# A decoder layer on one core: a fixed order of ScalarE and VectorE where attention begins, an earlier start of the first norm's sums, and another order in the closing chain

## The chip, the core and the metric

One core of a Trainium2 chip runs the whole layer in one launch. The metric is device time in microseconds (us), the median of several executions. The engines are TensorE (PE, matrix products), VectorE (DVE), ScalarE (ACT), GpSimd (POOL) and SyncE (SP, whose queue issues most transfers). Each executes its own instructions strictly in the order in which they were laid down, and waits at the first one whose inputs or buffers aren't ready.

## The reference

One decoder layer on 512 tokens of width 1024, all in 32-bit floats:

```python
cs = silu(c);  shift1, scale1, gate1, shift2, scale2, gate2 = split(cs @ w_ada + b_ada, 6)
h = rmsnorm(x, norm1_g) * (1 + scale1) + shift1
qa, ka, va, qd, kd, vd, ga, gd = split(h @ w_in)
out_a = sliding_window_attention(qa, ka, va, sinks)      # 8 heads, 2 key heads, window 128, ALiBi
out_d = diff_attention(qd, kd, vd, lambda)               # 4 heads, two softmax maps each, ALiBi
merged = sigmoid(ga) * (out_a @ w_branch_swa) + sigmoid(gd) * (out_d @ w_branch_diff)
x = x + gate1 * (merged @ w_out)
h2 = rmsnorm(x, norm2_g) * (1 + scale2) + shift2
x = x + gate2 * conv_ffn(h2)                             # up 1024 -> 2 x 2816, conv of 3, GELU, down
out = rmsnorm(x, final_g)
```

## The kernel before

Products are made to near 32-bit accuracy from two halves of each operand: a rounded high part (written by ACT, a cast or scaled copy) and the low part, the rest (written by DVE, a subtraction). A product is three matmuls: high by high, high by low, low by high. `split_pair` (L105) does it for a weight tile, `keep_v`, `stack` and `evac` for results that leave PSUM; `stack` puts the high and low half of one 64-row head above each other, so that one matmul multiplies both. Where a block is under `tc.manual_schedule(engines=...)`, the engines named run its instructions in the order of the text; elsewhere a scheduler orders them by priority and a model of their times, and `tc.issue_after(ins)` ties what a block issues on the engine of `ins` behind it.

**The opening** (L199 to L390, a fixed order on all engines). SP loads x in four quarters, then for each of eight slices k of the width two slabs of `w_ada` (the `adaw` tiles) and one of the first weights (`w0`). ACT squares each quarter of x, DVE folds the square in two, and `sums` (L289) adds over the partitions on PE, with a matrix of ones, into `stat`. `csb` is silu(c) spread over all partitions, copied from PSUM by two DVE copies (L253, L298). The shift's and scale's row sums are DVE multiply-and-reduce instructions (`mod_rows`, L259); for slice 0 the scale's is made by PE instead (`head_mod`, L279). ACT loads the root's table (`root_table`, L165), takes the root (L304), DVE finishes it (L306 on), PE turns it to a row (L312), and `scale_x`, `mod` and `h_tile` make h (L322, L357, L328). `keep_warm` puts products of constants into PE's idle time. Then PE multiplies slice after slice (`mm_k`, L339 and L342) into eight PSUM banks `acc[0..7]`: key (0), two query pairs (1, 2), values (3, 4, 6, 7 for the token blocks), window values (5). In the last slice the order of the banks is written out, so that they end one after the other.

**Where attention begins** (L434 on). ACT and DVE empty the eight banks: `keep_v(3)`, four copies of the key (L443) and two subtractions (L445), the first query pair (`stack`, L415 on ACT, L418 on DVE), copies of the key's low part, `vaT`; these are in a fixed order. The second query pair and the other three `keep_v` are not. PE's order is fixed: `fill(n)` does n steps (three matmuls each) of a queue of projections still to be done, the first two being query pairs 2 and 3 from weight tiles `wqa2` and `wqa3`, and between fills come the attention steps: `swa_scores` (L540, two calls for a pair; maxima on DVE, L545), `swa_softmax`, `swa_transpose`, `swa_values`. `SWA_FILL` lists the fills between them: the first before the first scores, the second between the two calls. Scores use the three banks tagged `s`, projections the two tagged `f`, transposes the two tagged `t`; `acc` holds the same banks before. `load_tile` issues a tile's transfer and its cast and low part; `prefetch` keeps one or two tiles ahead.

**Merge and output projection** (L884 to L1190). `add_merge(j)` finishes merged column block j on DVE (L913, L914 and a split). `load_rows` loads eight slabs of `w_out` (`wo`), multiplies each with the gate on DVE (L961) and splits it. The projection's eight accumulators (`oc`, L1186 to L1190) take the same PSUM banks as the merges' sums.

**The closing chain** (`last_rows`, L1671 on, fixed order on all engines). For the last two rows of tokens, u = 0 and 1, the half that is still open is multiplied by the gate (`last_mul`, L1648), added (`last_add`, L1651), squared (`last_square`, L1656), the root is taken (`root_start`, `root_end`), and both halves are scaled and written out (`last_final` L1664, `last_scale2` L1668). Row 1 is done in two quarters, c0 and c1, since PE ends with c1 in a bank of its own, `dY[1]`.

Of the kernel before, what the change touches and what calls it, by code (L numbers as in the profile page):

```python
# [8 lines left out]
F32 = mybir.dt.float32  # L9
# [5 lines left out]
P = 128  # L15
# [19 lines left out]
VA_AT = 5  # L35
SWA_FILL = (1, 2, 6, 2, 2, 2, 2, 3)
DIFF_FILL = (3, 2, 4, 2)
# [6 lines left out]
def kernel(  # L44
# [207 lines left out]
    nc.vector.tensor_mul(cb, bsc1, n1g)  # L252
    nc.vector.tensor_copy(csb[:, :S], acc[0])  # L253

# [19 lines left out]

    NB = P

    def head_mod(a0, a1):
# [6 lines left out]
    stat = acc[6][:, : NT * NB].rearrange("p (t n) -> p t n", n=NB)  # L284
    keep_warm(2)

    def sums(p):
        for t in range(NT):
            nc.tensor.matmul(  # L289
                stat[:, t], sqs[p][:, t * P : (t + 1) * P], ones[:, :NB], start=p == 0 and t == 0, stop=True,  # L290
                skip_group_check=True,
            )

    sqs = [pp.tile([P, 2 * S], F32, tag="sq", bufs=4, name=f"sq{p}") for p in range(KT // 2)]
    for p in range(KT // 2):
        nc.scalar.activation(sqs[p], xT[:, p], AF.Square)
        if p == 3:
            nc.vector.tensor_copy(csb[:, S:], acc[1])  # L298
        nc.vector.tensor_add(sqs[p][:, :S], sqs[p][:, :S], sqs[p][:, S:])
# [9 lines left out]
    rstd_end(rst, ms, r0, NT, pp)  # L309
    head_mod(0, 6)  # L310
    for t in range(NT):
        nc.tensor.transpose(acc[7][:, t * P : (t + 1) * P], rst[:, t : t + 1].to_broadcast([P, P]), ident)  # L312
# [6 lines left out]
    ALL = slice(0, S)  # L319

# [33 lines left out]
    HALVES = (slice(0, S // 2), slice(S // 2, S))  # L354
    scale_x(0, HALVES[0])
    m = mods[0]
    nc.vector.tensor_scalar(m[:, 0:1], acc[3][:, 0:1], n1g[:, 0:1], cb[:, 0:1], ALU.mult, ALU.add)  # L357
    nc.vector.tensor_add(m[:, 1:2], m[:, 3:4], bsh[:, 0:1])
    scale_x(0, HALVES[1])
# [49 lines left out]

    def stack(dst, src, scale, js=(0, 1), soon=True):  # L410
        with tc.high_priority(offset=HP) if soon else ExitStack():
            sc = [scale if isinstance(scale, float) else scale[own] for own, _ in halves]
            for j in js:
                own = halves[j][0]
                nc.scalar.activation(dst[own, j], src[own], AF.Copy, scale=sc[j])  # L415
            for j in js:
                own, other = halves[j]
                nc.vector.scalar_tensor_tensor(  # L418
                    dst[other, j], src[own], sc[j], dst[own, j].bitcast(F32), ALU.mult, ALU.subtract
                )  # L420
# [12 lines left out]

    def keep_v(i):  # L434
        t = TOKENS[i] * P
        evac(*(v[:, :, t : t + P] for v in vv), acc[i].rearrange("p (h d) -> p h d", d=P))

    man = ExitStack()
    man.enter_context(tc.manual_schedule(engines={nc.vector.engine, nc.scalar.engine}))
    keep_v(3)  # L440
    for j, (own, other) in enumerate(halves):
        for to in (own, other):
            nc.scalar.copy(ka[to, j, 0], acc[0][own])  # L443
    for j, (own, _) in enumerate(halves):
        nc.vector.tensor_sub(ka[own, j, 1], acc[0][own], ka[own, j, 0].bitcast(F32))  # L445
# [20 lines left out]


    def load_tile(n, name):
        r = raw_tile([P, KT, P], name)
        nc.sync.dma_start(r, w_tiles[n])  # L470
        return split_pair(r, [P, KT, P], name)

# [126 lines left out]
    def add_q(i):  # L599
        def q(wts):  # L600
            o = fbank(f"pqa{i}")
            yield from steps(o, wts, hT, KT)
            stack(qa[:, i], o, qsc[:, i : i + 1])

        units.append((lambda: load_tile(TILE_QA + i, f"wqa{i}"), q))

# [159 lines left out]
    ada = ada_rows()  # L766
    add_q(2)
    add_q(3)
# [95 lines left out]
    tdall = gpart(2, [P, 3, S], "tdall")  # L864
    tds = {}

# [26 lines left out]
    def add_merge(j):  # L893
# [14 lines left out]
        def branch(wts):  # L908
            o = sbank(f"pB{j}")
            rhs = [[vv[b][:, k] for k in range(4)] for b in range(2)]  # L910
            yield from steps(o, wts, rhs, 4, cl=slice(j % 2 * P, j % 2 * P + P))
            td = tds[j]
            nc.vector.scalar_tensor_tensor(td, td, 1.0, o, ALU.add, ALU.mult)  # L913
            nc.vector.tensor_add(td, td, ta[:, j])  # L914
            split(mgh[j], mgl[j], td)
# [755 lines left out]
    def last_rows(todo):  # L1671
# [132 lines left out]
```

## Time and profile before

| | us |
|---|---|
| median of 3 runs | 684.09 |
| lowest, highest | 683.17, 686.54 |
| profiled execution, whole | 684.12 |
| its span, first to last instruction | 682.3 |
| busy in it: PE, DVE, ACT, POOL | 670.2, 567.7, 403.7, 66.1 |

The profiled execution's time is 1.8 us more than its span. PE's busy time counts pipelined matmuls from start to a modelled end, so it hides short waits between them; where PE waits is better read from how many matmuls lie in a stretch.

### The profile page before, as it was taken

To read this page: it belongs to the slowest core of one execution; us is meant where nothing else is said; L and a number is where in the kernel's file an instruction comes from. 1 tells how busy PE (TensorE), PEld (TensorE's weight loads), DVE (VectorE), ACT (ScalarE), POOL (GpSimd) and SP (SyncE) were. 2 spreads that over 40 slices of the span, in tenths; PEclk is the share of its full clock that TensorE was granted. 3 is DMA by queue.
4 is the path that set the end of the run, shared out by engine and by line. 5 is a ranking of instruction groups with operands and counts; after the bars stand their busy time and mean duration, and the time that the engine had idled before them with its cause. 6 is when DMAs were issued, how large, how long until landed. Compare 5 with 4: busy or idle time off the path is not lost.

```text
span 682.3 us, 10835 instructions
## 1 busy us (share of the span) xinstructions
PE 670.2 (98%) x4053; PEld 594.3 (87%) x4053; DVE 567.7 (83%) x1049; ACT 403.7 (59%) x703; POOL 66.1 (10%) x74
## 2 busy tenths in 40 slices
PE   8999999999999999999999999999999999999995
PEld 7887787888888888878899999999999998888884
DVE  5986887789887388973689998888888999979997
ACT  6678878565654233332498565565556666656665
POOL 2000000001000000000020120111110003440300
PEclk9999999999999999999999999999999999999998
DMA  9961322354254289757473998787867658996903
GB/s 359 418 218 35 124 62 94 123 155 130 93 180 155 80 291 304 263 128 270 144 125 97 215 218 213 185 194 178 215 159 189 149 185 189 195 204 188 166 1 124
DMA packets 71077, 119.68 MB, mean 175 GB/s; under 512 B 3952, under 2 KB 47728, under 8 KB 71024
## 3 DMA queue, kind: packets, MB, share of 16 engines
q1 hardware_dynamic: 52960, 95.04, 41.7%
q0 software_dynamic: 17776, 23.60, 21.4%
q8 instruction: 32, 0.52, 0.3%
q10 hardware_dynamic: 288, 0.34, 0.2%
q14 instruction: 21, 0.17, 0.1%
HBM read 116.87 MB, written 2.10 MB: 174 GB/s over the span
## 4 chain that ended last, share of the span: by engine, by line
PE 79%; DVE 8%; DMA 6%; issue 3%; ACT 3%; ACTq 0%; DVEq 0%
PE up L1130 33%; PE dc L1733 11%; DMA wgd<-in_w_tiles_dram 3%; PE av L342 3%; DMA wo<-in_w_out_dram 2%; PE oc L1186 2%; PE oc L1187 2%; PE oc L1190 2%; PE pga L108 2%; PE pga L110 2%; PE pga L109 2%; PE sd L637 2%; PE aqa L339 1%; PE pq L108 1%; PE pk L108 1%
## 5 line engine op out<-in xcount | busy, mean ns | idle before, releaser
L1130 PE MATMUL up<-t,m_whi 128*128 128x256 f32 x512 | 93.1, 283 | 0.0
L1130 PEld LDWEIGHTS up<-t,m_whi 128*128 128x128 f32 x512 | 79.9, 192 | 0.0
L1130 PE MATMUL up<-t,m_wlo 128*128 128x256 f32 x256 | 72.4, 283 | 0.0
L1130 PE MATMUL up<-bh,p_whi 128*128 128x256 f32 x232 | 65.7, 283 | 0.0
L1130 PE MATMUL up<-bl,p_whi 128*128 128x256 f32 x232 | 65.7, 283 | 0.0
L1130 PE MATMUL up<-bh,p_wlo 128*128 128x256 f32 x232 | 65.7, 283 | 0.0
L1130 PEld LDWEIGHTS up<-t,m_wlo 128*128 128x128 f32 x256 | 49.2, 192 | 0.0
L1130 PEld LDWEIGHTS up<-bh,p_whi 128*128 128x128 f32 x232 | 44.5, 192 | 0.0
L1130 PEld LDWEIGHTS up<-bl,p_whi 128*128 128x128 f32 x232 | 44.5, 192 | 0.0
L1130 PEld LDWEIGHTS up<-bh,p_wlo 128*128 128x128 f32 x232 | 44.5, 192 | 0.0
L1033 POOL DMA_DIRECT2D s<-in_w_up_dram x21 | 27.0, 1365 | 158.2 <-DMA s<-in_w_up_dram 110.3
L1061 ACT CAST m_whi<-s 128x1024 fp32r<-128x1024 f32 x31 | 32.4, 1046 | 15.7 <-DVE s L1055 9.1
L732 DVE CUSTOM_DVE_ANT_0 ra<-ra,csb 128x1024 f32<-128x1024 f32 x32 | 38.6, 1221 | 1.6 <-DMA ra<-in_w_ada_t_dram 1.5
L1065 DVE TENSOR_TENSOR m_wlo<-s,m_whi 128x1024 fp32r<-128x1024 f32 x31 | 37.8, 1219 | 1.3 <-ACT m_whi L1061 1.3
L1130 PE MATMUL up<-t,p_whi 128*128 128x256 f32 x176 | 32.2, 283 | 0.0
L662 ACT ACTIVATE sd<-sd,dmx 128x128 f32<-128x128 f32 (+3 forms) x32 | 17.8, 557 | 20.7 <-DVE dmx L660 16.5
L1130 PEld LDWEIGHTS up<-t,p_whi 128*128 128x128 f32 x176 | 27.4, 192 | 0.1
L1061 ACT CAST p_whi<-wa 128x1024 fp32r<-128x1024 f32 x18 | 18.8, 1042 | 12.6 <-PE up L1130 5.4
L141 POOL TENSOR_TENSOR r<-ms,mhalf 128x4 f32<-128x4 f32 x4 | 5.3, 1323 | 215.5 <-DVE ms L137 215.5
L1137 ACT ACTIVATE gT<-a,cols 128x512 f32<-128x512 f32 x22 | 17.6, 812 | 13.4 <-DVE a L1172 13.0
L1065 DVE TENSOR_TENSOR p_wlo<-wa,p_whi 128x1024 fp32r<-128x1024 f32 x18 | 22.0, 1223 | 4.0 <-ACT p_whi L1061 3.8
L1130 PE MATMUL up<-t,p_wlo 128*128 128x256 f32 x88 | 24.9, 283 | 0.0
(519 smaller groups left out, 2055.7 us busy)
## 6 DMA issues: line engine op xcount, KB each, us to landing
ra<-in_w_ada_t_dram SPq DMA_DIRECT2D x32, 512.0 KB, 4.0
wa<-in_w_up_dram SPq DMA_DIRECT2D x22, 512.0 KB, 4.2
s<-in_w_up_dram SPq DMA_DIRECT2D x21, 512.0 KB, 4.5
s<-in_w_up_dram POOLq DMA_DIRECT2D x21, 512.0 KB, 7.2
adaw<-in_w_ada_t_dram SPq DMA_DIRECT2D x15, 512.0 KB, 10.0
a<-in_w_up_dram SPq DMA_DIRECT2D x11, 512.0 KB, 4.9
b<-in_w_down_dram SPq DMA_DIRECT2D x10, 512.0 KB, 4.0
w<-in_w_first_dram SPq DMA_DIRECT2D x8, 512.0 KB, 9.9
```

The lines of the kernel that those rows point to most:

```text
L108: nc.tensor.matmul(o, lh, rh, start=start, stop=False)
L109: nc.tensor.matmul(o, lh, rl, start=False, stop=False)
L110: nc.tensor.matmul(o, ll, rh, start=False, stop=stop)
L342: nc.tensor.matmul(acc[i], ht[:, t : t + P], wts[k][w][:, S:], start=start, stop=stop)
L662: nc.scalar.activation(pm[m], pm[m], AF.Exp, bias=mx[:, m : m + 1], scale=slope, accum_out=lsum[:, m : m + 1])
L732: nc.vector.tensor_tensor_reduce(r, r, csb, 1.0, 0.0, ALU.mult, ALU.add, late_mod[:, idx : idx + 1])
L1033: nc.gpsimd.dma_start(dst, upblock(*blk), accum_op=ALU.add)
L1061: nc.scalar.copy(W[J, name][0], R[J, SRC[name]])
L1065: nc.vector.tensor_sub(lo, R[J, SRC[name]], hi.bitcast(F32))
L1130: nc.tensor.matmul(o[u], w[:, k, cu], b[:, k], start=name in ("p1", "m5", "p2") and k == 0 and x == 0, stop=k == 3 and x == 2, skip_group_ ...
L1137: nc.scalar.activation(grow(j), av[J][:, u], AF.Identity, bias=cv[:, 66 + j : 67 + j], scale=cv[:, 44 + j : 45 + j])
L1733: nc.tensor.matmul((bank2[u] if o is None else o)[:, sl], a[:, q, cu], b[:, q, sl], start=first_mm and x == 0, stop=last_mm and x == 2, sk ...
```

## The change

At the start, the first copy of `csb` moves behind the second quarter's sums and the second behind the root's table load; the last quarter of x is squared, folded and summed in halves; slice 0's shift is summed by two half instructions (`shift_half`), one ahead of the root and one behind it; the scale's head sum goes five parts before and three behind the transposes; three warm-up products go. In the last slice bank 0 ends before bank 3.

Where attention begins, the two query weight tiles, the key, the first query pair, the high parts of the second and of two value blocks get a fixed order on ACT and DVE, sorted by what the first scores need; the second query pair's and the three remaining values' low parts come behind the first softmax. The first two fills are 2 and 1 instead of 1 and 2. The multiply of `wo6` goes behind the last two merges. In the closing chain `last_add(1)` and the square of row 1's quarter move ahead.

```diff
-SWA_FILL = (1, 2, 6, 2, 2, 2, 2, 3)
+SWA_FILL = (2, 1, 6, 2, 2, 2, 2, 3)
...
     nc.vector.tensor_mul(cb, bsc1, n1g)
-    nc.vector.tensor_copy(csb[:, :S], acc[0])
...
-    keep_warm(2)
-
-    def sums(p):
-        for t in range(NT):
+    def sums(p, ts=range(NT)):
+        for t in ts:
...
     for p in range(KT // 2):
-        nc.scalar.activation(sqs[p], xT[:, p], AF.Square)
-        if p == 3:
-            nc.vector.tensor_copy(csb[:, S:], acc[1])
-        nc.vector.tensor_add(sqs[p][:, :S], sqs[p][:, :S], sqs[p][:, S:])
-        sums(p)
+        for hf in range(2) if p == 3 else (None,):
+            sl = ALL if hf is None else HALVES[hf]
+            sq, xx = (a.rearrange("p (a s) -> p a s", a=2)[:, :, sl] for a in (sqs[p], xT[:, p]))
+            nc.scalar.activation(sq, xx, AF.Square)
+            nc.vector.tensor_add(sq[:, 0], sq[:, 0], sq[:, 1])
+            sums(p, range(NT) if hf is None else range(2 * hf, 2 * hf + 2))
+        if p == 1:
+            nc.vector.tensor_copy(csb[:, :S], acc[0])
     root_table(sqs[3][:, 0:1])
-    mod_rows(0, 1)
+    nc.vector.tensor_copy(csb[:, S:], acc[1])
+
+    def shift_half(hf):
+        a = adaw[0][:, 1, hf * S : (hf + 1) * S]
+        nc.vector.tensor_tensor_reduce(
+            a, a, csb[:, hf * S : (hf + 1) * S], 1.0, 0.0, ALU.mult, ALU.add, mods[0][:, 4 + hf : 5 + hf]
+        )
+
+    shift_half(0)
...
     rstd_end(rst, ms, r0, NT, pp)
-    head_mod(0, 6)
+    shift_half(1)
+    head_mod(0, 5)
...
-    head_mod(6, KT)
+    head_mod(5, KT)
...
-            for i in (3, 0, 1, 5, 2, 4, 6, 7):
+            for i in (0, 3, 1, 5, 2, 4, 6, 7):
...
-    keep_warm(4)
+    keep_warm(3)
...
-    nc.vector.tensor_add(m[:, 1:2], m[:, 3:4], bsh[:, 0:1])
+    nc.vector.scalar_tensor_tensor(m[:, 1:2], m[:, 4:5], m[:, 5:6], bsh[:, 0:1], ALU.add, ALU.add)
...
+    first_tiles = [load_tile(TILE_QA + i, f"wqa{i}") for i in (2, 3)]
+    nc.scalar.copy(ka[lower, 0, 0], acc[0][lower])
+    nc.scalar.copy(ka[upper, 1, 0], acc[0][upper])
+    nc.vector.tensor_sub(ka[lower, 0, 1], acc[0][lower], ka[lower, 0, 0].bitcast(F32))
+    nc.vector.tensor_sub(ka[upper, 1, 1], acc[0][upper], ka[upper, 1, 0].bitcast(F32))
     keep_v(3)
-    for j, (own, other) in enumerate(halves):
-        for to in (own, other):
-            nc.scalar.copy(ka[to, j, 0], acc[0][own])
-    for j, (own, _) in enumerate(halves):
-        nc.vector.tensor_sub(ka[own, j, 1], acc[0][own], ka[own, j, 0].bitcast(F32))
-    stack(qa[:, 0], acc[1], qsc[:, 0:1])
-    for j, (own, other) in enumerate(halves):
-        nc.scalar.copy(ka[other, j, 1], ka[own, j, 1])
-    nc.scalar.copy(vaT, acc[5])
+    nc.scalar.activation(qa[lower, 0, 0], acc[1][lower], AF.Copy, scale=qsc[lower, 0:1])
+    nc.vector.scalar_tensor_tensor(
+        qa[upper, 0, 0], acc[1][lower], qsc[lower, 0:1], qa[lower, 0, 0].bitcast(F32), ALU.mult, ALU.subtract
+    )
+    nc.scalar.copy(ka[upper, 0, 0], acc[0][lower])
+    nc.scalar.copy(ka[upper, 0, 1], ka[lower, 0, 1])
+    nc.scalar.activation(qa[upper, 0, 1], acc[1][upper], AF.Copy, scale=qsc[upper, 0:1])
+    nc.vector.tensor_copy(ka[lower, 1, 0], acc[0][upper])
+    nc.vector.tensor_sub(ka[lower, 1, 1], acc[0][upper], ka[lower, 1, 0].bitcast(F32))
+    nc.vector.scalar_tensor_tensor(
+        qa[lower, 0, 1], acc[1][upper], qsc[upper, 0:1], qa[upper, 0, 1].bitcast(F32), ALU.mult, ALU.subtract
+    )
+    stack(qa[:, 1], acc[2], qsc[:, 1:2], soon=False, low=False)
+    keep_v(6, (0,))
+    vat_copy = nc.scalar.copy(vaT, acc[5])
     man.close()
-    stack(qa[:, 1], acc[2], qsc[:, 1:2], soon=False)
-    keep_v(4)
-    keep_v(6)
-    keep_v(7)
+    keep_v(4, (0,))
+    keep_v(7, (0,))
...
-    with tc.issue_after(tiles[KT - 1].ins):
-        prefetch(1)
+    with tc.issue_after(vat_copy.ins):
         fill(SWA_FILL[0])
-    swa_scores(0, 0)
-    with tc.issue_after(pairs[0].last.ins):
-        fill(SWA_FILL[1])
-        swa_scores(0, 2)
-    with tc.issue_after(pairs[0].last.ins):
+        swa_scores(0, 0)
+        with tc.issue_after(pairs[0].last.ins):
+            fill(SWA_FILL[1])
+            swa_scores(0, 2)
+    with tc.issue_after(pairs[0].last.ins), tc.issue_after(vat_copy.ins):
         swa_softmax(0)
+        keep_v(6, (1,))
+        stack(qa[:, 1], acc[2], qsc[:, 1:2], high=False)
+        keep_v(4, (1,))
+        keep_v(7, (1,))
...
-            nc.vector.scalar_tensor_tensor(td, td, 1.0, o, ALU.add, ALU.mult)
+            merged.append(nc.vector.scalar_tensor_tensor(td, td, 1.0, o, ALU.add, ALU.mult))
...
-    with tc.issue_after(recent[0].ins), tc.issue_after(recent[1].ins):
-        wo = [load_rows(wout, 0, "wo0", g1b)]
-    wo += [load_rows(wout, k, f"wo{k}", g1b) for k in range(1, KT)]
+    wo = []
+    for k in range(KT):
+        with ExitStack() as place:
+            for b in recent if k == 0 else merged[-2:] if k == 6 else ():
+                place.enter_context(tc.issue_after(b.ins))
+            wo.append(load_rows(wout, k, f"wo{k}", g1b))
...
         last_mul(1, dW[1])
+        last_add(1)
         r0 = root_start(s0, D, bp, part[0])
         rs0 = bp.tile([P, 1], F32, tag="rs2", bufs=4, name="rse0")
         root_end(rs0, *r0, bp)
-        last_add(1)
+        s1 = last_square(1, c0)
         last_scale2(0, rs0, nc.sync)
-        s1 = last_square(1, c0)
```

In `keep_v` and `stack` the new arguments pick which of the two halves, high and low, are written; `load_tile` is unchanged but stands earlier in the text.

More of the change, by code (lines that the diff above doesn't have):

```diff
@@ L275 @@
     NB = P
+    ALL = slice(0, S)
     def head_mod(a0, a1):
@@ L317 @@
     hfs, tiles = {}, {}
-    ALL = slice(0, S)
     def scale_x(k, sl=ALL):
@@ L408, with stack @@
     halves = ((lower, upper), (upper, lower))
-    def stack(dst, src, scale, js=(0, 1), soon=True):
+    def stack(dst, src, scale, soon=True, high=True, low=True):
         with tc.high_priority(offset=HP) if soon else ExitStack():
             sc = [scale if isinstance(scale, float) else scale[own] for own, _ in halves]
-            for j in js:
+            for j in range(2) if high else ():
                 own = halves[j][0]
                 nc.scalar.activation(dst[own, j], src[own], AF.Copy, scale=sc[j])
-            for j in js:
+            for j in range(2) if low else ():
                 own, other = halves[j]
@@ L432, with keep_v, load_tile @@
     vaT = big.tile([P, S], F32, tag="sq2", name="vaT")
-    def keep_v(i):
+    def keep_v(i, parts=(0, 1)):
         t = TOKENS[i] * P
-        evac(*(v[:, :, t : t + P] for v in vv), acc[i].rearrange("p (h d) -> p h d", d=P))
+        hi, lo = (v[:, :, t : t + P] for v in vv)
+        src = acc[i].rearrange("p (h d) -> p h d", d=P)
+        if 0 in parts:
+            nc.scalar.copy(hi, src)
+        if 1 in parts:
+            nc.vector.tensor_sub(lo, src, hi.bitcast(F32))
+    def load_tile(n, name):
+        r = raw_tile([P, KT, P], name)
+        nc.sync.dma_start(r, w_tiles[n])
+        return split_pair(r, [P, KT, P], name)
@@ L603, in q @@
             stack(qa[:, i], o, qsc[:, i : i + 1])
-        units.append((lambda: load_tile(TILE_QA + i, f"wqa{i}"), q))
+        units.append((None, q))
     def add_head(h):
@@ L766 @@
     ada = ada_rows()
-    add_q(2)
-    add_q(3)
+    for i in (2, 3):
+        add_q(i)
+        loaded.append((first_tiles[i - 2], units.pop()[1]))
     add_head(0)
     add_head(1)
-    with tc.issue_after(tiles[KT - 1].ins):
-        prefetch(1)
+    with tc.issue_after(vat_copy.ins):
         fill(SWA_FILL[0])
-    swa_scores(0, 0)
-    with tc.issue_after(pairs[0].last.ins):
-        fill(SWA_FILL[1])
-        swa_scores(0, 2)
-    with tc.issue_after(pairs[0].last.ins):
+        swa_scores(0, 0)
[3 more added lines that the diff above has]
+    with tc.issue_after(pairs[0].last.ins), tc.issue_after(vat_copy.ins):
         swa_softmax(0)
+        keep_v(6, (1,))
+        stack(qa[:, 1], acc[2], qsc[:, 1:2], high=False)
+        keep_v(4, (1,))
+        keep_v(7, (1,))
         lp = cpool.tile([P, 2, 64], F32, name="lp")
@@ L864 @@
     tdall = gpart(2, [P, 3, S], "tdall")
-    tds = {}
+    tds, merged = {}, []
     g1b = gpart(4, [P, D], "g1b")
```

6 lines of the change are left out of this document (1 added, 5 removed).

## The prediction

> **What bounds the kernel now.** I read the page first, then the busy time by stretches, then the timeline of the four places that the change touches.
>
> ```profile
> span 682.3 us, 10835 instructions
> PE 79%; DVE 8%; DMA 6%; issue 3%; ACT 3%; ACTq 0%; DVEq 0%
> ```
>
> The chain that ended last is 79% TensorE (PE), so a microsecond counts only where PE waits. The windows view, for PE alone, says where that is; a count includes matmuls that overlap the edge of a window.
>
> ```profile
> 15.18:59.01 43.83, 43.83 (x192) 1.00 0.72 279
> 59.01:61.29 2.28, 2.10 (x13) 1.00 0.00 0
> 62.66:64.36 1.70, 1.22 (x10) 1.00 0.00 0
> 68.46:69.24 0.78, 0.39 (x3) 1.00 0.00 0
> 69.58:70.50 0.92, 0.92 (x10) 1.00 0.60 85
> 74.84:76.11 1.27, 1.27 (x10) 1.00 0.06 19
> 70.50:301.78 231.28, 231.28 (x1179) 1.00 0.50 159
> 303.12:674.90 371.78, 371.77 (x2537) 1.00 0.72 172
> ```
>
> Columns: length, PE busy, granted clock, DMA share, GB/s. PE is packed from 15.18 to 59.01 (192 matmuls in 43.83: 0.228 us each), from 70.50 to 301.78 and from 303.12 to 674.90. What can be won lies before 15.18, between 59 and 70.5, in the hole from 301.78 to 303.12, and behind 674.90. The profiled execution took 684.12 us for its span of 682.3, so 1.8 us lie around it; it is 0.03 above the median of 684.09. The sum is made against 684.12.
>
> **The opening.** These rows of the timeline carry it.
>
> ```profile
> 3.07 0.60 SPq L189 DMA_DIRECT2D adaw<-in_w_ada_dram  x1
> adaw<-in_w_ada_dram SPq DMA_DIRECT2D x1, 512.0 KB, 7.9
> 5.00 2.04 ACT L296 ACTIVATE sq<-xT 128x1024 f32<-128x1024 f32 x2
> 6.54 0.69 DVE L253 COPY csb<-aka 128x512 f32<-128x512 f32 x1 [0.45 <-PE aka L245]
> 7.88 3.84 PE L289 MATMUL av<-ones,sq 128*128 128x128 f32 x32 [0.50 <-DVE sq L299]
> 8.48 1.06 ACT L296 ACTIVATE sq<-xT 128x1024 f32<-128x1024 f32 x1 [0.18 <-DMA xT<-in_x_t_dram]
> 9.56 1.28 ACT L165 ACT_TABLE_LOAD   x1
> 10.18 1.22 DVE L259 CUSTOM_DVE_ANT_0 adaw<-adaw,csb 128x1024 f32<-128x1024 f32 x1
> 10.85 0.20 ACT L165 ACTIVATE warm<-sq 128x1 f32<-128x1 f32 x1
> 11.82 0.26 ACT L304 ACTIVATE r<-av,eps 128x4 f32<-128x4 f32 x1 [0.77 <-PE av L289]
> 12.12 0.16 DVE L306 TENSOR_SCALAR ms<-av 128x4 f32<-128x4 f32 x1 [0.71 <-ACT r L304]
> 13.01 0.65 PE L312 MATMUL av<-ident,rst 128*128 128x128 f32 x4
> 13.50 0.61 PE L279 MATMUL av<-cs,adaw 128*128 128x128 f32 x4
> 14.15 0.28 DVE L357 TENSOR_SCALAR mod<-av,cols,cb 128x1 f32<-128x1 f32 x1
> ```
>
> The sums of squares are 32 PE records at about 0.11 us (3.84 over 32), unbroken from 7.88, and the root waits 0.77 us for them. They start late because the 0.69 us copy L253 stands before the first add. Moved behind the second add, it lets the first add run when the first square is done, near 6.1 (two squares take 2.04 from 5.00); PE then starts the sums near 6.9, a microsecond sooner. The two warm-up matmuls taken out there cost nothing. The last squares cannot start before 8.48, when x lands; in halves they end near 9.65 (two starts where there was one), the adds near 10.1, and PE, left with half a sum, ends near 11.1. The table load follows the squares, 9.65 to 10.95, and its filler runs to 11.15. VectorE (DVE) now does copy L298 (priced as L253, 0.69) and the first half of the shift's row sum (half of 1.22 and a start, 0.7) behind the adds, to 11.4. So `ms` starts at 11.42 instead of 12.12: 0.70 sooner. The other half of the row sum, 0.7 again, lies in DVE's wait for the transposes (they start 0.89 behind `ms`, 12.12 to 13.01, and take 0.5) and ends about when they do.
>
> What is late next is the head sum L279. It reads the weights that land at 10.9 (3.07 plus 7.9). Five of eight parts now go ahead of the transposes, three behind: six records instead of four. With the transposes at 12.31 it ends near 13.65, where before it ended at 14.11 (13.50 + 0.61). The scale L357 follows at 13.68 instead of 14.15, h and PE's first product with it: **0.47 us**. Bounds: 0.70 if the head sum doesn't end last; 0.3 if the halves cost another 0.2. The packed stretch behind only shifts.
>
> [...] The rows show the table load taking 1.28 us and the next activation 0.01 us behind it. [...]
>
> **Where attention begins.** PE's order there is fixed in both kernels; the change fixes the order of ScalarE (ACT) and DVE.
>
> ```profile
> 57.60 1.41 DVE L445 TENSOR_TENSOR ka<-aka,ka 64x512 fp32r<-64x512 f32 x2 [1.57 <-ACT ka L443]
> 62.32 0.74 DVE L418 SCALAR_TENSOR_TENSOR qa<-aqa,qsc,qa 64x512 fp32r<-64x512 f32 x1 [0.93 <-ACT qa L415]
> 66.17 1.88 DVE L402 TENSOR_TENSOR vvl<-av,vvh 128x512 fp32r<-128x512 f32 x3
> 67.97 1.21 DVE L105 TENSOR_TENSOR wqa_l<-wqa,wqa_h 128x1024 fp32r<-128x1024 f32 x1
> 69.24 0.50 PE L110 MATMUL pqa<-hThA,wqa_l 128*128 128x512 f32 x1 [0.39 <-DVE wqa_l L105]
> ```
>
> Three waits, each priced by the same work without one. From 59.01 PE does three fills and eight score matmuls in 2.28; the same eight take 0.92 at 69.58 and three fills 0.68, so 0.68 is waiting. The wide eight at 62.66 take 1.70 against 1.27 at 74.84: 0.43. One fill at 68.46 takes 0.78 against 0.23: 0.55. Together 1.66.
>
> The first goes because the order is now by operand. DVE may read a bank only behind all earlier ACT reads of it (L445 waits 1.57 for four copies); with two copies ahead, the key's low parts start near 55.2 and end near 56.6, on a clock that is 0.47 ahead. Counting every half-height step of the new order at 0.6 to 0.75 (1.41 for two at 57.60, 0.74 at 62.32), the first head's operands are ready near 58.0 and the second's near 60.0. PE reaches them at 59.9 and 60.3, since two fills, not one, stand ahead; the margin is 0.3 us. The second wait goes because the second query's low halves (L418 at 62.32) no longer stand between the maxima and the score banks they free. The third goes because the weight low part runs at 52 to 54, where DVE had nothing, instead of 67.97. Moving the two tiles' loads in the text is no burden to SP's queue: the tile behind them was already being cast at 53.77 (row under rival (e)).
>
> What is late next: the second query's product needs the bank that the value copy frees. Its three low parts (1.88 us) and two query low parts (1.5) now run from about 64.0 (66.17 less what the waits and the opening gave back), and the needed one, fourth in that row, ends near 66.8. PE asks for it after both score groups, six fills and the turn of the values: 59.9 + 0.92 + 1.27 + 6 × 0.68, and 0.4 for four transposes (13.01 to 13.50), 66.6. I charge 0.2 of a possible 0 to 0.4. Net **1.46 us**, with bounds 1.1 and 1.66.
>
> **The hole at 301.78.**
>
> ```profile
> 301.24 1.23 DVE L961 TENSOR_TENSOR wo<-wo,g1b 128x1024 f32<-128x1024 f32 x1 [0.64 <-DMA wo<-in_w_out_dram]
> 302.39 0.68 DVE L913 SCALAR_TENSOR_TENSOR tdall<-tdall,pB 128x512 f32<-128x512 f32 x1
> 303.12 0.50 PE L1186 MATMUL oc<-wo_h,mg0h 128*128 128x512 f32 x1 [1.34 <-DVE tdall L913]
> ```
>
> The last merge L913, which frees a bank for the output projection, is queued behind L961, which waits for a DMA. The change puts the gate multiply of wo6 behind the last two merges. DVE was idle for 0.64 ahead of L961, from 300.6; the merge then ends near 301.25, before PE asks at 301.78. **1.34 us**, bounds 1.0 and 1.34. The multiply itself starts no later than its DMA allows plus 0.1, and wo6 is used tens of microseconds later. That DMA loop was released by PE earlier on, so I let it shift with PE.
>
> **The closing chain.**
>
> ```profile
> 674.00 0.16 DVE L161 RECIPROCAL r<-r 128x1 f32<-128x1 f32 x1
> 674.46 0.16 DVE L151 SCALAR_TENSOR_TENSOR rse<-rt,r 128x1 f32<-128x1 f32 x1
> 674.53 0.68 DVE L1651 TENSOR_TENSOR x<-x,pairs 128x512 f32<-128x512 f32 x1
> 675.32 0.42 DVE L1648 TENSOR_TENSOR pairs<-dc,g2row 128x256 f32<-128x256 f32 x1
> 678.57 0.38 ACTq L1669 DMA_DIRECT2D out_dram<-x  x1
> ```
>
> The add at 674.53 moves ahead of the root, into DVE's gap, and ends near 674.5; the reciprocal's 0.62 us to the end of `rse` follow, so the next multiply starts at 675.07 instead of 675.32. ACT's order changes with it: the square of the finished quarter now precedes the scaling of the first rows, which becomes about 0.5 us later and isn't last. The rest shifts by **0.25 us**; bounds 0 and 0.4.
>
> **Sum.** 0.47 + 1.46 + 1.34 + 0.25 = 3.52. 684.12 − 3.52 = 680.6. With all lower ends 2.4 (681.7), with all upper ends 4.1 (680.0).
>
> **The rivals.**
>
> (a) The bank for the second query's product comes late. If DVE takes the softmax's normalisation ahead of that low part, PE waits 1.8 more at 66.5 and attention gives nothing: 682.1. For it: the softmax has priority over it. Against it: its exponentials must run first, and the low part stands ready meanwhile. 0.10.
>
> (b) The hole stays. L913 may stand behind another multiply waiting for its DMA, since the edge binds wo6 alone: 681.9. Against it: only one such wait, 0.64, stands near. 0.08.
>
> [...] 0.02.
>
> (d) The order isn't the one that the text says, because the parts outside the fixed block are still placed by the scheduler: 682.1 without attention's gain. 0.04.
>
> (e) Slower. Before, a third weight tile was cast ahead of attention; now its cast stands behind the copy of the values.
>
> ```profile
> 53.77 1.05 ACT L105 CAST w_h<-w 128x1024 fp32r<-128x1024 f32 x1 [0.66 <-PE av L342]
> 69.46 1.19 DVE L105 TENSOR_TENSOR w_l<-w,w_h 128x1024 fp32r<-128x1024 f32 x1
> 78.20 0.39 PE L108 MATMUL pq<-hThA,w_h 128*128 128x512 f32 x1
> ```
>
> So the prefetch is one tile shorter. That tile was complete at 70.65 and used at 78.20, 7.5 us of slack; after, it is used near 76.2. It decides from a completion later than 76.2, and the kernel ends later than before from 79.7 on. A unit is 24 matmuls, 5.5 us: one tile late by a unit gives 686.1, two give 691.6. Against it: even a cast that is 9 us later than 53.77 runs ahead of the old low part at 69.46. 0.06, of which 0.05 beyond 0.5%.
>
> **How the numbers follow.** The forecast has 0.70, the rivals 0.30. A difference of 0.5%, 3.42 us, is about what a measurement of this kernel can tell from no change, and the forecast's own 3.52 lies just beyond it: time below 680.67. Its bounds lie on both sides; I give the faster side 0.50 of its 0.70, as three of the four terms are holes seen in the rows, and a hole that closes closes whole. Rivals (a) to (d) and the rest of the forecast end within 0.5%, with what (e) leaves: 0.45. Slower is 0.05. The range runs from 679.1 (the upper ends, 680.0, and the 0.9 by which the lowest of the three runs, 683.17, lies below the median) to 682.5, which takes in the lower ends and (a) to (d).
>
> **What would show it.** Right: the first sums at 6.9, `ms` near 11.4, PE's first product near 14.7; no PE wait between 58.5 and 68; no wait of L1186 for L913; the last output issued near 675. Wrong: a PE wait for the value copy's low part, for a weight's low part after 75, or a new one in the long packed stretches.

## The result, and the profile after

The changed kernel takes 680.56 us (median of 8 runs, 680.29 to 680.95); the kernel before, over 8 runs, 683.85 (683.17 to 686.54). The ratio is 0.995, with a 95% interval of 0.994 to 0.9961. The forecast was 680.6, with a range of 679.1 to 682.5. The profiled execution took 680.29 us.

The page's first line and its chain that ended last, of the changed kernel:

```profile
span 678.4 us, 10826 instructions
PE 97%; DVE 1%; DMA 1%; ACT 0%; issue 0%; ACTq 0%
```

Before, TensorE (PE) held 79% of the chain, after 97%: nearly every wait of PE in the middle is gone. The windows view, PE alone (columns as in the prediction: length, PE busy, granted clock, DMA share, GB/s):

```profile
14.89:58.69 43.80, 43.80 (x192) 1.00 0.76 295
58.69:61.14 2.45, 2.45 (x15) 1.00 0.00 0
61.84:62.78 0.94, 0.94 (x9) 1.00 0.00 0
68.10:69.02 0.92, 0.92 (x9) 1.00 0.00 0
73.24:74.28 1.04, 1.04 (x11) 1.00 0.00 0
296.00:301.00 5.00, 5.00 (x28) 1.00 0.32 105
301.00:671.00 370.00, 370.00 (x2532) 1.00 0.72 172
```

The wide scores that took 1.70 (at 62.66) now take 0.94, and those of the next pair 1.04 where they took 1.27. Where the hole would lie now, from 299.9 to 301.3, PE is busy throughout. The timeline of the changed kernel at the four places:

```profile
7.37 3.78 PE L287 MATMUL av<-ones,sq 128*128 128x128 f32 x32
9.66 1.28 ACT L165 ACT_TABLE_LOAD   x1
10.95 0.20 ACT L165 ACTIVATE warm<-sq 128x1 f32<-128x1 f32 x1
11.55 0.16 DVE L316 TENSOR_SCALAR ms<-av 128x4 f32<-128x4 f32 x1 [0.24 <-ACT r L314]
12.92 0.83 PE L279 MATMUL av<-cs,adaw 128*128 128x128 f32 x6
13.79 0.28 DVE L365 TENSOR_SCALAR mod<-av,cols,cb 128x1 f32<-128x1 f32 x1 [0.25 <-PE av L279]
14.89 0.50 PE L351 MATMUL av<-whi,hThA 128*128 128x512 f32 x1 [0.46 <-ACT hThA L337]
...
59.71 0.75 DVE L473 SCALAR_TENSOR_TENSOR qa<-aqa,qsc,qa 64x512 fp32r<-64x512 f32 x1
60.05 1.26 PE L562 MATMUL sw<-ka,qa 128*128 128x128 f32 x8
65.96 1.29 DVE L449 TENSOR_TENSOR vvl<-av,vvh 128x512 fp32r<-128x512 f32 x2
66.80 0.63 PE L486 MATMUL pva<-ident,vaT 128*128 128x128 f32 x4 [0.42 <-DVE vvl L449]
73.17 1.22 DVE L105 TENSOR_TENSOR w_l<-w,w_h 128x1024 fp32r<-128x1024 f32 x1
76.35 0.39 PE L108 MATMUL pq<-hThA,w_h 128*128 128x512 f32 x1
...
298.04 0.68 DVE L939 SCALAR_TENSOR_TENSOR tdall<-tdall,pB 128x512 f32<-128x512 f32 x1
298.86 1.23 DVE L987 TENSOR_TENSOR wo<-wo,g1b 128x1024 f32<-128x1024 f32 x1
299.78 0.39 PE L1215 MATMUL oc<-wo_h,mg0h 128*128 128x512 f32 x1
...
671.50 0.42 DVE L1677 TENSOR_TENSOR pairs<-dc,g2row 128x256 f32<-128x256 f32 x1
674.73 0.38 ACTq L1698 DMA_DIRECT2D out_dram<-x  x1
```

The first scores start without a wait, but their second half still comes late: VectorE (DVE) ends the last low part of the query (first row of the second group) at 60.46, the fifth of the eight matmuls starts at 60.61, and the eight take 1.09 between starts (60.05 to 61.14) where they take 0.92 at 68.10. The profile's idle column doesn't show this 0.17, since the modelled ends cover it. One wait is new: the transposes of the value copy wait 0.42 for the low part of the value tile in bank 6. The last merge (L939, L913 before) runs ahead of the multiply of wo6 (L987, L961 before) and ends 1.06 before PE comes to its bank.

Where the time went is read by setting the start of the same matmul in two executions against each other, a shift. Its steps from before to after:

```
 first product   -0.29    (15.18 -> 14.89; -0.32 a few matmuls on, up to 59)
 attention       -1.52    (-0.32 at 59.46 -> -1.84 at 78, then constant up to 299)
 hole at 301     -1.68    (-1.84 -> -3.52)
 303 to 674      -0.05
 closing         -0.28
 sum             -3.8     (684.12 -> 680.29)
```

The medians differ by 3.29 only. The experiments show why.

### The profile page after: what moved, and what is told of

It reads as the page before. It is cut to its first block, busy times and chain, and to the rows that moved or that the text cites. A ratio compares the mean times of both kernels' runs of the same rounds, so it can differ in the third digit from the quotient of the medians.

```text
span 678.4 us, 10826 instructions
## 1 busy us (share of the span) xinstructions
PE 669.2 (99%) x4047; PEld 594.8 (88%) x4047; DVE 569.2 (84%) x1054; ACT 402.2 (59%) x702; POOL 66.0 (10%) x74
## 4 chain that ended last, share of the span: by engine, by line
PE 97%; DVE 1%; DMA 1%; ACT 0%; issue 0%; ACTq 0%
PE up L1159 33%; PE dc L1762 15%; PE av L351 3%; PE pga L108 2%; PE pga L110 2%; PE pga L109 2%; PE pgd L110 2%; PE oc L1215 2%; PE pgd L108 2%; PE oc L1216 2%; PE oc L1219 2%; PE pgd L109 2%; PE aqa L348 2%; PE sd L659 2%; PE pq L108 1%; PE pk L108 1%
```

## The experiments

**Each part alone.** Four kernels, each the kernel before with one part of the change. The opening alone:

```diff
+(the edits up to and with keep_warm(3) and m[:, 1:2]; nothing behind them)
```

> The kernel before with the opening's edits alone (sums of squares in their own place, last quarter of x and the shift's row sum in halves, head sum 5 and 3, three warm products); attention, hole and closing chain as before. Theory (each part moves its own place): first product about 14.9 against 15.18, every later matmul 0.3 sooner up to the first scores, and about 0.3 at the end: 0.9995 of the kernel before, inside what timing can tell. Rival (what the opening gains is lost at the first wait behind it, since the casts of the first projections set it): the shift is back to 0 behind 62. Side question: TensorE's records at full pace from about 4.8 (as before) or from about 7.0 (as in the changed kernel); if from 4.8, the first sums at 6.9 and the mean square at 11.42 as forecast.

Attention alone:

```diff
+(the edits of SWA_FILL, the last slice's banks, keep_v, stack, the fixed order, first_tiles, issue_after(vat_copy))
```

> The kernel before with the fixed order of casts, copies, first weight tiles and first scores alone. Theory: no wait ahead of the first scores nor ahead of the wide scores behind them, a new wait of about 0.4 at the transposes of the value copy; shift of the matmuls 0 up to 59 and -1.5 from 76 on; end 1.5 sooner, 0.998 of the kernel before. Rival (the opening and attention's order need each other: without the earlier opening ScalarE reaches the casts late): less than 1.0.

The hole's edge alone:

```diff
+merged.append(nc.vector.scalar_tensor_tensor(td, td, 1.0, o, ALU.add, ALU.mult))
...
+            for b in recent if k == 0 else merged[-2:] if k == 6 else ():
+                place.enter_context(tc.issue_after(b.ins))
```

> The kernel before with the one edge alone: the seventh output weight tile (wo6) waits for the merges of the last two heads. Theory: the wait of TensorE at 301.6 goes, the matmuls behind it come 1.5 to 1.7 sooner, and so does the end: 0.9976 of the kernel before. Rival (the merges came in time in the changed kernel only because attention's start had moved the casts on VectorE): shift 0 behind 303, or the wait comes back elsewhere before 330.

The closing chain alone:

```diff
+        last_add(1)
         r0 = root_start(s0, D, bp, part[0])
...
-        last_add(1)
+        s1 = last_square(1, c0)
         last_scale2(0, rs0, nc.sync)
-        s1 = last_square(1, c0)
```

> The kernel before with the closing chain's order alone. Theory: last matmul unmoved at 674.6, last output issued 0.25 to 0.28 sooner than 678.57; the time 0.25 less, which timing can't tell from nothing. Rival (the reordered steps only trade places, and the last issue waits for the same multiply): 678.57 within 0.05.

The kernel before ran beside them 31 times: 683.31 (682.34 to 685.57).

```
              median (range)            ratio to before, 95%        shift against the first profile of before at
                                                                    first product   58     86     290    309    last output
 e1 opening   682.56 (682.22-684.69)    0.9999 (0.9987 to 1.001)        -0.04     -0.04  -0.04  -0.04  -1.72   -1.71
 e2 attention 681.75 (680.73-683.08)    0.9975 (0.9963 to 0.9987)       +0.31     +0.30  -1.22  -1.12  -2.48   -2.46
 e3 edge      682.56 (682.01-683.04)    0.9986 (0.9977 to 0.9995)       +0.40     +0.40  +0.38  +0.67  -0.95   -0.99
 e4 closing   683.34 (682.58-684.07)    0.9998 (0.9988 to 1.0007)       +0.12     +0.11  +0.07  +0.05  -0.95   -1.21
```

(The ratios are the record's own, not quotients of these medians.) Attention alone gives −1.52 between 58 and 86, as it does in the whole change, though it starts 0.31 late here: it doesn't need the earlier opening. e1 can't show more on that, as its shift is near nothing. It had 0.3 as its forecast, but in its execution the last quarter of x landed at 8.76, 0.30 later than in that of before (8.46); counted from there, its first product comes 0.34 sooner (6.38 against 6.72). By timing alone no gain of the opening is shown.

e3's ratio missed its forecast, 0.9976, by a tenth of a percent. The four ratios add up to 0.42% less, within the interval of the whole.

But the columns hold two surprises. The opening's start differs by 0.4 between executions of one and the same code. And the hole at 301 shrinks in all four, though only e3 has the edge: by 1.68 in e1, 1.36 in e2, 1.00 in e4. (The 0.29 that e3 loses between 86 and 290 goes nearly all in one step at 143, as does the 0.1 of e2; ScalarE waited 2.4 and 2.2 there for the landing of another weight tile, `wga`, and 1.2 in the kernel before; the chain between the two wasn't followed.) The timeline of e1, e4 and e3 there (scaling of wo6; last merge; PE's matmul that needs its bank; in e3 also the scaling of wo5, first row):

```profile
299.28 1.23 DVE L969 TENSOR_TENSOR wo<-wo,g1b 128x1024 f32<-128x1024 f32 x1 [0.54 <-DMA wo<-in_w_out_dram]
300.42 0.68 DVE L921 SCALAR_TENSOR_TENSOR tdall<-tdall,pB 128x512 f32<-128x512 f32 x1
301.57 0.39 PE L1194 MATMUL oc<-wo_h,mg0h 128*128 128x512 f32 x1
```

```profile
300.34 1.23 DVE L961 TENSOR_TENSOR wo<-wo,g1b 128x1024 f32<-128x1024 f32 x1 [0.49 <-DMA wo<-in_w_out_dram]
301.48 0.68 DVE L913 SCALAR_TENSOR_TENSOR tdall<-tdall,pB 128x512 f32<-128x512 f32 x1
302.21 0.50 PE L1186 MATMUL oc<-wo_h,mg0h 128*128 128x512 f32 x1 [0.38 <-DVE tdall L913]
```

```profile
296.39 1.23 DVE L961 TENSOR_TENSOR wo<-wo,g1b 128x1024 f32<-128x1024 f32 x1 [1.60 <-DMA wo<-in_w_out_dram]
301.37 0.68 DVE L913 SCALAR_TENSOR_TENSOR tdall<-tdall,pB 128x512 f32<-128x512 f32 x1
301.97 1.22 DVE L961 TENSOR_TENSOR wo<-wo,g1b 128x1024 f32<-128x1024 f32 x1
302.29 0.40 PE L1189 MATMUL oc<-wo_h,mg0h 128*128 128x512 f32 x1
```

Up to 303 e4 executes the same instructions as the kernel before; its scaling of wo6 starts at 300.34, that of before at 301.24. Both start as the load lands, and the merge follows 1.14 to 1.15 later. So the hole isn't a fixed cost: it is the landing of one load, which differs from execution to execution, less PE's own place. In e3 the load lands latest of all, at 301.84, and PE doesn't wait. What e4 was made for, 0.28 between PE's last matmul and the last output, is in its trace (below) and too small for the timing.

**The edge taken out.**

```diff
-            for b in recent if k == 0 else merged[-2:] if k == 6 else ():
...
+    with tc.issue_after(recent[0].ins), tc.issue_after(recent[1].ins):
+        wo = [load_rows(wout, 0, "wo0", g1b)]
+    wo += [load_rows(wout, k, f"wo{k}", g1b) for k in range(1, KT)]
```

> The changed kernel without the edge that holds wo6 behind the merges. Found so far: in four executions without that edge the scaling of wo6 on VectorE began within 0.06 of its load's landing (298.8 to 301.2), the merge stood behind it, and TensorE's hole at 301.6 was 1.68, 1.00, 0.32 and 0. Theory (the hole is the landing time of one load, which moves from execution to execution, less TensorE's own place): the hole is back, between 0 and 1.9 by where the load lands; the merge starts within 0.1 of the end of wo6's scaling; the executions spread over about 2 us instead of 0.7, and their median lies 0.5 to 1.0 above the changed kernel's (ratio to before about 0.9965 instead of 0.995). Rival (a fixed cost of 1.5, as forecast from the one trace): every execution 1.5 above the changed kernel's, spread 0.7.

(The 1.00 in that list is what e4 gained on the kernel before; its own hole was 0.68.) Measured: 680.98 (680.36 to 682.34), 0.4 above the changed kernel and so just under the theory's 0.5 to 1.0; spread 2.0. The kernel before took 683.04 beside it, so it lies 2.06 below that, where the whole change lay 3.29 below. In its profile the load landed at 298.48:

```profile
298.50 1.22 DVE L987 TENSOR_TENSOR wo<-wo,g1b 128x1024 f32<-128x1024 f32 x1 [0.53 <-DMA wo<-in_w_out_dram]
299.64 0.68 DVE L939 SCALAR_TENSOR_TENSOR tdall<-tdall,pB 128x512 f32<-128x512 f32 x1
300.38 0.50 PE L1212 MATMUL oc<-wo_h,mg0h 128*128 128x512 f32 x1
```

The merge stands behind the load again, and PE comes 0.20 late; the rival's 1.5 in every execution is out. The five executions without the edge lost 1.68, 0.68, 0.32, 0.20 and 0 here. In all five the merge starts 1.16 to 1.17 behind wo6's landing; in the nine with the edge it starts 5.00 behind the landing of wo5, the load before. The edge moves the merge 1.7 to 1.9 forward on that chain; it doesn't cut it from the loads.

**The value tile's low part first.**

```diff
         swa_softmax(0)
-        keep_v(6, (1,))
+        with tc.high_priority(offset=HP):
+            keep_v(6, (1,))
```

> The changed kernel with the low part of the value tile of bank 6 raised in priority, so that VectorE does it between the two low parts of the query and not behind them and the second row maximum. Theory (the wait of 0.42 at the transposes of the value copy is that low part alone): it starts at about 64.9 instead of 65.96, ends ahead of 66.3, the wait is gone and the matmuls behind 67 come 0.4 to 0.6 sooner up to 69, but 0.1 to 0.3 of it is paid back at the third query product and the wide scores; end 0.3 to 0.5 sooner, 680.1 to 680.3. Rival (the value copy's transposes wait for something else that comes at the same time, or the scores behind them take the wait over): shift back to 0 behind 76.

Measured: 680.54 (680.47 to 680.82); shift against the changed kernel −0.26 from the opening, −0.11 at 68, +0.24 from 73 on: half a microsecond lost in this execution, not won; the timing can't tell it from the changed kernel's 680.56. The transposes no longer wait; the product behind them does, for the low part of the next bank:

```profile
67.19 0.50 PE L108 MATMUL pqa<-hThA,wqa_h 128*128 128x512 f32 x1 [0.63 <-DVE vvl L449]
```

The theory was right on what the first wait was, and wrong that one low part was all: VectorE (DVE) is behind here by two. The rest went at 71, where ScalarE had put a weight cast between the two halves of the softmax and copied the values late.

**One group of products ahead of the first scores.**

```diff
-SWA_FILL = (2, 1, 6, 2, 2, 2, 2, 3)
+SWA_FILL = (1, 2, 6, 2, 2, 2, 2, 3)
```

> The changed kernel with one group of products ahead of the first scores and two behind them (1, 2 instead of 2, 1). Theory (the operands come just in time: ready at 60.0, TensorE there at 60.05): first scores wait 0.5 to 0.7, the ones behind them wait less or nothing, net 0.3 to 0.7 later, 0.4 to 0.7 of the 1.52 lost. Rival (the order of the casts does it all, the two numbers nothing): shift within 0.1 of 0 behind 62.

```profile
59.89 1.48 PE L562 MATMUL sw<-ka,qa 128*128 128x128 f32 x8 [0.30 <-DVE ka L472]
```

Measured: 681.23 (680.63 to 681.55). The scores wait, and the shift goes from +0.06 to +0.75: 0.69 of the 1.52 hang on these two numbers. With both groups ahead the first head's operands are in time; the second head's are still 0.17 late, so of the margin of 0.3 that the prediction had nothing is left.

**The old order of casts.**

```diff
     keep_v(3)
+    for j, (own, other) in enumerate(halves):
+        for to in (own, other):
+            nc.scalar.copy(ka[to, j, 0], acc[0][own])
...
```

(and so on, in place of the sorted block from `ka[lower, 0, 0]` to `qa[lower, 0, 1]`)

> The changed kernel with the casts and copies of the first key and query tiles in the order of the kernel before (all key copies on ScalarE, value's high part first), the two groups of products, early weight tiles and late low parts as changed. Theory (the order of the casts counts beside the two groups): the first scores wait 0.5 to 1.2 for the last copy or low part, since seven casts of ScalarE stand ahead of them instead of six with the reads of one bank taken in turn; end 0.5 to 1.2 later than the changed kernel's. Rival (moving one group of products was enough): shift within 0.1 of 0 behind 62.

Measured: 680.36 (680.3 to 681.11); shift −0.12 at 60, +0.06 from 73 to 126. (At 141 this execution lost 0.8 more: ScalarE waited 2.9 for `wga`, the tile that cost e3 0.29; its 681.11 is the slowest of the five.) Only 0.18 is lost by the casts in the trace, and none by timing; that is nearer to the rival: their sorted order, which I took for the heart of this part, is worth an eighth of it.

**VectorE's whole stretch by PE's needs.**

```diff
-        swa_softmax(0)
-        keep_v(6, (1,))
-        stack(qa[:, 1], acc[2], qsc[:, 1:2], high=False)
-        keep_v(4, (1,))
+        with tc.manual_schedule(engines={nc.vector.engine}):
+            swa_maxima(0)
+            keep_v(6, (1,))
+            keep_v(4, (1,))
+            stack(qa[:, 1], acc[2], qsc[:, 1:2], soon=False, high=False)
+        swa_softmax(0, False)
         keep_v(7, (1,))
...
```

> The changed kernel with VectorE's order from 63.9 to 72.4 written for TensorE's needs: both row maxima of the first softmax, then the low parts of the value tiles of banks 6 and 4, then the query low parts; the score copies of the first two score tiles of pair 1 two behind each half of the softmax; the third query's low part behind it all. Theory (raising one low part only moved the wait to the next bank; TensorE needs banks 6 and 4 by 66.4 and 66.7, the query by 67.4, the score banks by 72.5): transposes of the value copy without a wait, third product at 66.7 instead of 67.30, next scores at 67.4 instead of 68.10, and 0.5 to 0.76 sooner from there to the end; 679.9 to 680.1 against the changed kernel run again beside it. Rival (VectorE has no room: a later wait for the softmax or a score bank takes all of it): shift 0 behind 76.

`swa_maxima(0)` holds both row maxima of the first softmax. The changed kernel ran again beside it:

> The changed kernel once more, beside the others of this call. Theory: 680.3 to 680.9 with a spread of 0.7; the load of wo6 lands anywhere from 298.4 to 299.4 and TensorE doesn't wait at 301; the opening's way from the last quarter of x to the mean square takes 3.04 to 3.08 again. Rival (the first profile was a lucky execution): a hole of 0.3 or more at 301, or 3.4 and more in the opening.

Measured: 680.34 (680.26 to 680.96, 6 runs) against 680.54 (680.32 to 681.88, 6 runs); the two can't be told apart. In the trace the plan works where it was made: from +0.30 (the opening) to −0.45 behind 67, 0.75 won, no wait at the transposes or the third product. Then it is given back: 0.27 at 70.6, where the other transposes wait for ScalarE's copy of the values, and 0.24 at 98. The profiled execution also lost 0.70 at the output projection, with the edge in place, since wo5 landed late there (scaling of wo5; merge; PE):

```profile
294.65 1.23 DVE L1006 TENSOR_TENSOR wo<-wo,g1b 128x1024 f32<-128x1024 f32 x1 [2.04 <-DMA wo<-in_w_out_dram]
299.63 0.68 DVE L958 SCALAR_TENSOR_TENSOR tdall<-tdall,pB 128x512 f32<-128x512 f32 x1
300.37 0.50 PE L1234 MATMUL oc<-wo_h,mg0h 128*128 128x512 f32 x1 [0.39 <-DVE tdall L958]
```

So no version here is shown to beat the changed kernel. The changed kernel's second profile has no wait at 301 and 3.06 from x's last quarter to `ms`, as its theory said. Its load of wo6 landed at 297.64, sooner than the 298.4 to 299.4 of the theory, and one of its six runs, 681.88, lay outside the 680.3 to 680.9.

**The second weight tile cast late.**

```diff
-    first_tiles = [load_tile(TILE_QA + i, f"wqa{i}") for i in (2, 3)]
...
+    with tc.issue_after(tiles[KT - 1].ins):
+        prefetch(1)
+        fill(SWA_FILL[0])
```

> The changed kernel without the early casts of the second weight tile: only the first of the two query weight tiles is cast ahead of the fixed order, the second where the products ask for it. Theory (a cast of 1.22 put in VectorE's way delays everything behind it): the low part stands between the score copies at about 62.5, the row maxima come 1.2 later, the value copy's transposes and the third product wait 0.8 to 1.2 more; end 0.8 to 1.2 later, and this and the two groups (0.69) and the casts' order (0.18) then make up more than the whole 1.52. Rival (VectorE's gap covers it): 0 to 0.3.

Measured: 683.58 (682.34 to 685.51), 3.04 above the changed kernel beside it and a loss of 3.5 in the trace, three times the theory's. The timeline, and the windows view, of this kernel:

```profile
63.30 1.23 DVE L105 TENSOR_TENSOR wqa_l<-wqa,wqa_h 128x1024 fp32r<-128x1024 f32 x1 [1.26 <-ACT wqa_h L105]
68.72 0.63 PE L485 MATMUL pva<-ident,vaT 128*128 128x128 f32 x4 [2.31 <-DVE vvl L449]
```

```profile
58.69:66.40 7.71, 7.71 (x41) 1.00 0.11 31
66.40:68.70 2.30, 0.01 (x1) 1.00 0.30 123
68.72:69.94 1.22, 1.22 (x7) 1.00 0.00 0
69.95:73.36 3.41, 3.41 (x14) 0.50 0.02 5
73.37:75.00 1.63, 1.63 (x13) 1.00 0.00 0
```

The low part stands between the score copies, where the theory put it, but DVE first waits 1.26 for the cast on ScalarE, with everything queued behind it: PE's wait grows by 1.9 instead of 0.8 to 1.2. Then PE is clocked down: 1.2 after it has started again its granted clock falls to 0.50 and stays there for 3.41 us. Wide matmuls come 0.427 apart where they were 0.227, and another 1.55 is gone.

**The low parts early.**

```diff
-    stack(qa[:, 1], acc[2], qsc[:, 1:2], soon=False, low=False)
-    keep_v(6, (0,))
     vat_copy = nc.scalar.copy(vaT, acc[5])
     man.close()
-    keep_v(4, (0,))
-    keep_v(7, (0,))
+    stack(qa[:, 1], acc[2], qsc[:, 1:2], soon=False)
+    keep_v(4)
+    keep_v(6)
+    keep_v(7)
...
         swa_softmax(0)
-        keep_v(6, (1,))
-        stack(qa[:, 1], acc[2], qsc[:, 1:2], high=False)
-        keep_v(4, (1,))
-        keep_v(7, (1,))
```

> The changed kernel with the second query's casts and the last three value tiles where the kernel before has them: behind the value copy, high and low together, not held behind the first scores. Theory (VectorE works on low parts while TensorE waits for its scores): the second query's low parts (1.5) stand ahead of the first score copies, the second set of scores waits 0.7 to 1.5 for a score bank, but the wait at the value copy's transposes is gone; net 0.3 to 1.0 later. Rival (only VectorE's sum of work counts, whatever its order): within 0.2 of the changed kernel.

```profile
62.79 1.33 PE L562 MATMUL sw<-ka,qa 128*128 128x256 f32 x8 [0.34 <-DVE qa L426]
71.80 0.55 PE L601 MATMUL tp<-ident,st 128*128 128x128 f32 x3 [0.39 <-ACT va L487]
```

Measured: 681.17 (680.64 to 681.48). The second scores come 0.74 later; the wait at the value copy goes and gives 0.76 back; then the transposes at 71.8 wait for ScalarE and 0.62 is lost again: net 0.58, in the theory's range. A late wo5 adds 0.27 at 301 in that execution.

Taken out one at a time, attention's edits cost 0.69, 0.18, 3.5 and 0.58, together three times the 1.52 that they give together: they are fitted to each other, and a price of one of them holds only with the others in place.

## Why the prediction was right, point by point

**Opening, 0.47 forecast.** The mechanism held: sums sooner, root sooner, then the head sum last. In the pair of profiles it gave 0.29 to 0.32. The term was mis-sized by steps of about 0.1: `ms` at 11.55, not 11.42, and from the scale to the first product 1.10 (13.79 to 14.89) where before had 1.03. The first sums came at 7.37, not 6.9, but that cost nothing: in the ten executions with the new opening `ms` follows the landing of x's last quarter by 3.04 to 3.09, whether the sums begin at 6.58 or at 7.37. With the old one the sums themselves set the root in three of four: they ran unbroken for 3.84 from 7.88, 7.99 and 8.29.

PE's records start 0.21 apart in all fourteen profiles and change to 0.11 at some time between 4.7 and 7.1 (before 4.9, after 7.1). With the new opening, the way from the landing of x's last quarter to the first product is 6.38 to 6.44 in ten executions, whether the pace changes at 4.7 or at 7.1. With the old one it was 6.72 and 6.48 where the pace changed at 4.9, and 6.98 and 7.05 where it changed at 6.6 and 6.3. (The 6.48 is e2's, where x landed last of all, at 9.02, and the sums paused for it.) So the opening gives 0.05 to 0.65, on average 0.4, within the bounds of 0.3 to 0.7 on average, and one pair of profiles can't size it. Which of the opening's edits gives how much wasn't tried. The landing itself moves from 8.19 to 9.02, whatever the kernel.

**Attention, 1.46 forecast, 1.52 measured, and the same alone.** The sum is right, its parts are not. The wide scores were priced by the same eight at 74.84, 1.27; those held a wait too, since without one they take 0.94. So the second wait gave 0.75, not 0.43. The first gave 0.50, not 0.68: the second head's operands were ready at 60.46, not near 60.0, and the 0.17 stayed. The stretch from 68 to 78 gave another 0.36 that no term had, most of it in the scores at 74.84. (The prediction says fill both for one matmul, 0.23, and for a step of three, 0.68; its sums use the right one each time.) Against that, the bank that the value low parts hold came late one step sooner than argued: at the transposes of the value copy, not at the second query's product. There DVE took both query low parts and the second row maxima first, and 0.61 was lost where 0.2 was charged. That wait is one of the prediction's own signs of being wrong, and it came. The sum held all the same, since what the second wait and the last stretch gave beyond their terms covers what the first wait and the bank took. The wait for the weight's low part gave 0.52, as forecast (0.55).

**Hole, 1.34 forecast, 1.68 measured.** Two things were off. The idle column counts from a modelled end of the pipelined matmul; by starts, 301.39 to 303.12 is 1.73 where 0.23 is usual, 1.50, and the matmuls behind a wait come 0.34 and 0.24 apart, another 0.2. And the hole was read from one execution as a fixed cost; without the edge it is 0 to 1.68, on average over five 0.58. The edge's worth by timing is 0.14% (0.05 to 0.23%), about 0.95 us.

**Closing, 0.25 forecast, 0.28 measured.** From the start of PE's last matmul to the last issue of an output it takes 3.99 in the four executions with the old order and 3.71 to 3.72 in the ten with the new: 0.27 to 0.28. The next multiply came at 671.50 with PE 3.56 earlier, as forecast.

**The total.** 3.52 was forecast from 684.12 and 3.83 came in the profile: the hole was undersized by 0.34 and the opening oversized by about 0.15, and the rest gave 0.06, 0.03 and 0.05 more. That the median was met to 0.04 has a second cause: the profiled executions lie 0.27 above (before) and 0.27 below (after) the medians, which differ by 3.29. The one on which the sum stood had the longest hole of five, so part of its 1.68 wasn't there to be won in the others. Two errors cancel, which is luck.

**The rivals.** (a) came in part: the bank was late, one step sooner and at a third of the price, 0.61, but not for its reason. DVE took the softmax's normalisation only at 68.10, behind that low part (65.96). (b) in part: with the edge the merge still waits for wo5, and two of nine executions lost 0.70 and 0.27. For the 0.02 of (c) no run shows a cause: the table load at 9.66 takes 1.28, to 10.94, and the next activation starts at 10.95. Each of the changed kernel's six table loads takes 1.28, the next activation starts 0.01 behind it, and five of them start 0.02 behind ScalarE's work before. (d) in part: the text has the value low part ahead of the query's, the scheduler had them the other way round. (e) didn't decide, but its working was wrong. The third tile's cast came at 62.20, 8.4 later, and its low part at 73.17, not ahead of 69.46: it ends at 74.39 and is used two matmuls behind 76.35, a margin of 2.4 where I saw over 5. And of its two times only 691.6 is more than 0.5% above the kernel before, so one tile late by a unit, 686.1, doesn't belong in the 0.05 for slower.

## What to carry to other kernels

A wait on a DMA read from one profile is a sample, not a price: look in several executions at how the landing moves, and let the work that others wait for run ahead of the instruction that waits for it (the spread was 2.0 without the edge, 0.7 and 1.6 with it). To price a wait by "the same work without one", make sure that the reference has none, by the sum of its instructions' own spacing. Where an engine is behind by two pieces of work, moving one of them forward only moves the wait: list all deadlines of the stretch, and its other engines', before reordering it.

## What the runs showed of the hardware

In e11 a wait of PE of 2.3 us (2.70 between starts) was followed by a granted clock of 0.50, from 69.95 to 73.36 and so from 1.2 after the wait, at a cost of 1.55. Behind waits of 0.4 to 1.7 that was not seen in any of these profiles. The time at which PE's records change from 0.21 apart to 0.11 varies from run to run: 4.7 to 7.1 in fourteen profiles, with PE's first matmul at 1.13 in each. The granted clock's column shows 1.00 ahead of the change all the same (1.13 to 4.80 in the kernel before, 1.13 to 7.00 in the changed one).
